# A hybrid retention, RG-LRU and PEER layer on one core: other start addresses for the activation tiles

## The chip, the core and the metric

The kernel runs on one core of a Trainium2 chip. The core has five engines, each with its own instruction queue: TensorE (PE in the profile; its weight loads are PEld), VectorE (DVE), ScalarE (ACT), GpSimd (POOL) and SyncE (SP), which here only issues DMAs. Operands lie in the on-chip memory SBUF, 128 partitions wide; a tile is a range of bytes that begins at the same address in every partition. Matmul results go to PSUM. The metric is the time of one execution on the device in microseconds (us), the median of several runs.

## What is computed

The reference is one layer over 256 tokens of width 2048 with all weights in float32, and a final norm:

```python
def hybrid_layer(h, mem, ...):
    xn = rms_norm(h, mix_norm_g)
    proj = xn @ w_in                                   # 2048 x 6144
    q, k, v, g, xb, yb = jnp.split(proj, ...)
    ret = silu(g) * head_group_norm(chunkwise_retention(rotary(q), rotary(k), v), ret_gn_g)
    lru = rg_lru_group(xb, yb, ...)
    h = h + jnp.concatenate([ret, lru], axis=-1) @ w_out
    h = h + memory_cross_attention(rms_norm(h, ...), rms_norm(mem, ...), w_xq, w_xk, w_xv, w_xo)
    h = h + peer_ffn(rms_norm(h, ffn_norm_g), peer_w_q, peer_sub_keys, peer_u, peer_v)
    return h

def peer_ffn(xn, w_q, sub_keys, u_tab, v_tab):
    sub_scores = ...                                   # 8 heads, 2 halves, 128 keys
    vals, ids = lax.top_k(sub_scores, 16)
    top_sc, pos = lax.top_k(all 256 sums of the two halves, 16)
    eid, gate = ..., softmax(top_sc)                   # 128 experts of 16384 per token
    act = gelu(einsum('td,tkd->tk', x, u_tab[eid]))
    return einsum('tk,tkd->td', gate * act, v_tab[eid])
```

Before it starts, the host only reorders the weights; all arithmetic is on the chip.

## The kernel before

**Float32 products from halves.** Each weight comes in tiles of 128 x 1024 floats (512 KB), loaded by SyncE into a ring of four buffers named `raw`. ScalarE rounds a tile to `hi` (L119, or L1076 in the last part), VectorE computes the remainder `lo` (L120, L1082), and TensorE multiplies both with an activation that is split in the same way. `raw`, `hi` and `lo` lie in the pool `ws` and begin 64 bytes past a multiple of 256.

**Two forms of product.** In `w_mms` (L128 and L131) the weight half is the stationary operand, 128 x 128 at a time, and the activation moves: 512 columns for `hi` (activation high and low part side by side), 256 for `lo`. A block of 128 outputs takes two tiles, 16 + 16 matmuls. `fold` adds the two halves of the result. In `xchunk` (L170 to L172) and `v_mms` (L939 to L941) the activation is stationary and 512 columns of the weight half move, three matmuls for each pair of operands, twelve for a tile.

**The stages, in order of time** (us from the start of the span, with the activation tile that each multiplies):

- 18 to 309: w_in, as 24 blocks for xb, yb and the gate (L128/L131) around 6 chunks for q, k and v (L170 to L172, 109 to 260), all with `xT`. The recurrence and the retention are woven in by `Weave.pump`, a few steps of side work after each weight tile.
- 309 to 517: w_xk (16 blocks) and w_xv (4 chunks) with `mT`.
- 517 to 609: w_out, 4 chunks with `cat`. 609 to 723: w_xq, 16 blocks with `hT`, and the attention. 723 to 822: w_xo, 4 chunks with `oT`.
- 822 to 921: w_pq, 16 blocks with `hT2`; `route` begins on VectorE as side work (top 16 of the scores, for token tile 0 and then 1).
- 921 to 1277: the first 6 chunks of U (L128/L131, 8 blocks each) with `xn`; the end of `route`, then `gbuild` and `compact`, which turn the choice into gate tables (L857 to L875) and lists.
- 1277 to 1898: V chunks 0 to 6 (16 tiles of 12 matmuls, L939 to L941) between the last 6 chunks of U. V multiplies with `ah` and `al`, the high and low part of the gated activations. This part has an order written out by step (`run`): the high half is made three steps ahead, the low half two, the load is issued six ahead.
- 1898 to 2115: V chunks 7 to 10, whose activations lie in `xe`, in the place of `xn`, which is no longer needed. 2115 to 2170: the last V chunk, with `ah` and `al` again, and the final norm.

From 1277 on, the chosen experts that the dense part leaves out are gathered by indirect DMAs from GpSimd (L1119) into a ring of four tiles `gat`, and VectorE multiplies (L1136) and adds (L1144) them as side work.

**What places a tile.** A pool takes its space where the pools before it end, and a tile within it where the tile before it ends, in steps of 32 bytes. The pool `rp` holds `cand`, `eq` and `gs` and ends where `pw` begins, which holds the big activation tiles (`xT`, `cat`, `oT`, `kq`, and above them `lt`, `kv`, `hT2`). Later the pool `pb` takes the place of `pw`: `act`, `foldu`, `key`, `work`, `gsp`, `sel`, `idx`, then `spt`, `spti`, `spi`, `spg`, and last `ah` and `al`. `mT`, `hT`, `xn` and `xe` share one place in the pool `b8`, below `rp`.

**What orders VectorE.** Outside the part with steps, a scheduler of the language orders each engine's instructions by what they depend on, byte range by byte range, starting from the order of the code. `gs` was a tile of its own; `r3` is a view of the tile `rt` whose first row `r3[:, 0]` holds the top values (`vals`) of both score halves, 16 for each of 16 score rows.

## Time and profile before

| | |
|---|---|
| runs | 2168.70, 2173.79, 2179.55 us; median 2173.79 |
| profiled execution | 2172.21 us, of which the span from first to last instruction is 2170.4 |
| mean granted TensorE clock | 0.982 of full speed |
| HBM | 540.94 MB read, 18.87 MB written |
| chain that ended last | TensorE 65%, VectorE 16%, DMA 12%, issue 4%, ScalarE 2% |

The next lines are from the second part of the page, which cuts the span into 40 slices of 54 us. A digit is a share in tenths, 9 is 90% or more; PEclk is the TensorE clock that was granted, DMA the mean busy share of the 16 DMA engines.

```profile
DVE  6847976744554558999987779999999999888885
PEclk9999999999999999999999989999999999999999
DMA  8665555566554457555676579999998999989864
```

VectorE and the DMA engines are far from full in the first half, but for the slices of `route`, and both near full from slice 24 on, where U, V and the gathers run together.

### The profile page before, as it was taken

Reading aid. Unit: us, or ns where it says so; the run is one execution under the profiler, and the core shown is the slowest. Engines: PE = TensorE matmul, PEld = TensorE weight load, DVE = VectorE, ACT = ScalarE, POOL = GpSimd, SP = SyncE. Lnnn points to the kernel's source line nnn. Section 1 sums busy time; section 2 is a strip of 40 time slices with the busy share of each in tenths; the row PEclk is TensorE's granted clock in tenths of the full one; section 3 lists DMA queues with packets and bytes.
Section 4 is the critical chain, followed back from the end, with each engine's and each line's share of the span. In section 5 each row is a group of like instructions: output and inputs, shape, how many; then the busy total and the mean of one; then the engine's idle time right before and its main releaser. Section 6 shows DMA issues by size and latency. Waiting matters only on the chain.

```text
span 2170.4 us, 29029 instructions
## 1 busy us (share of the span) xinstructions
PE 2074.1 (96%) x10452; PEld 1736.4 (80%) x10452; DVE 1702.6 (78%) x2422; ACT 1041.5 (48%) x1592; POOL 357.1 (16%) x210
## 2 busy tenths in 40 slices
PE   8999999999999999999999989989999999988998
PEld 6777788888888888888899878778788777766786
DVE  6847976744554558999987779999999999888885
ACT  6565344444544445454588834443434444333334
POOL 0302221000000000000000013332334233233211
PEclk9999999999999999999999989999999999999999
DMA  8665555566554457555676579999998999989864
GB/s 280 234 211 161 170 170 174 159 193 187 183 167 144 146 176 280 175 178 182 217 231 199 161 288 361 385 356 379 353 336 313 365 387 367 368 337 369 287 214 144
DMA packets 154870, 541.86 MB, mean 250 GB/s; under 512 B 17120, under 2 KB 44384, under 8 KB 136544
## 3 DMA queue, kind: packets, MB, share of 16 engines
q1 hardware_dynamic: 132832, 400.48, 54.5%
q0 software_dynamic: 21888, 139.48, 16.2%
q8 instruction: 82, 1.34, 0.2%
q14 instruction: 68, 0.56, 0.1%
HBM read 540.94 MB, written 18.87 MB: 258 GB/s over the span
## 4 chain that ended last, share of the span: by engine, by line
PE 65%; DVE 16%; DMA 12%; issue 4%; ACT 2%; POOL 0%; DVEq 0%; ACTq 0%; SPq 0%; POOLq 0%
PE U L128 9%; PE wb L128 6%; PE xc L171 6%; PE xc L172 6%; PE xc L170 6%; DMA raw<-in_V_dram 5%; PE U L131 5%; DMA raw<-in_U_dram 5%; PE acc L940 4%; DVE lo L120 4%; PE acc L939 4%; PE acc L941 4%; PE wb L131 3%; DVE lo L1082 3%; PE G L873 2%
## 5 line engine op out<-in xcount | busy, mean ns | idle before, releaser
L120 DVE TENSOR_TENSOR lo<-raw,hi 128x1024 fp32r<-128x1024 f32 x396 | 496.1, 1267 | 265.6 <-PE xc L171 141.0
L119 ACT CAST hi<-raw 128x1024 fp32r<-128x1024 f32 x396 | 415.1, 1050 | 292.8 <-PE xc L172 178.1
L1076 ACT CAST hi<-raw 128x1024 fp32r<-128x1024 f32 x272 | 285.7, 1051 | 410.6 <-DMA raw<-in_V_dram 202.8
L128 PE MATMUL U<-xn,hi 128*128 128x512 f32 x1536 | 383.9, 397 | 9.3 <-DVE foldu L1013 5.0
L1082 DVE TENSOR_TENSOR lo<-raw,hi 128x1024 fp32r<-128x1024 f32 x272 | 328.1, 1220 | 55.9 <-ACT hi L1076 37.8
L128 PEld LDWEIGHTS U<-xn,hi 128*128 128x128 f32 x1536 | 281.7, 190 | 67.5 <-DVE foldu L1013 5.7
L1119 POOL DMA_INDIRECT gat<-in_Us_dram,idx x72 | 123.3, 1713 | 701.7 <-DVE gat L1136 268.2
L131 PE MATMUL U<-xn,lo 128*128 128x256 f32 x1536 | 215.2, 288 | 18.8 <-DVE lo L1082 14.2
L131 PEld LDWEIGHTS U<-xn,lo 128*128 128x128 f32 x1536 | 202.1, 193 | 31.3 <-DVE lo L1082 18.4
L1119 POOL DMA_INDIRECT gat<-in_Vs_dram,idx x72 | 132.3, 1838 | 267.8 <-DVE hh L1144 235.5
L1144 DVE SCALAR_TENSOR_TENSOR hh<-gat,coef,hh 128x2048 f32<-128x2048 f32 x72 | 168.8, 2344 | 0.0
L1136 DVE SCALAR_TENSOR_TENSOR gat<-gat,h 128x2048 f32<-128x2048 f32 x72 | 164.4, 2283 | 0.0
L939 PE MATMUL acc<-hi,ah 128*128 128x512 f32 x384 | 153.0, 398 | 5.0 <-ACT hi L1076 3.4
L940 PE MATMUL acc<-lo,ah 128*128 128x512 f32 x384 | 154.5, 402 | 2.2 <-DVE lo L1082 2.0
L941 PE MATMUL acc<-hi,al 128*128 128x512 f32 x384 | 151.7, 395 | 0.0
L128 PE MATMUL wb<-hT,hi 128*128 128x512 f32 x448 | 113.9, 398 | 0.0
L128 PEld LDWEIGHTS wb<-hT,hi 128*128 128x128 f32 x448 | 81.3, 189 | 15.5
L939 PEld LDWEIGHTS acc<-hi,ah 128*128 128x128 f32 x384 | 72.6, 189 | 24.2 <-ACT hi L1076 3.9
L128 PE MATMUL wb<-xT,hi 128*128 128x512 f32 x368 | 90.3, 396 | 0.1
L940 PEld LDWEIGHTS acc<-lo,ah 128*128 128x128 f32 x384 | 72.7, 189 | 21.9 <-DVE lo L1082 5.2
L941 PEld LDWEIGHTS acc<-hi,al 128*128 128x128 f32 x384 | 72.8, 190 | 17.3
L940 PE MATMUL acc<-lo,xe 128*128 128x512 f32 x192 | 77.1, 401 | 9.7 <-DVE lo L1082 9.7
(404 smaller groups left out, 3659.2 us busy)
## 6 DMA issues: line engine op xcount, KB each, us to landing
raw<-in_U_dram SPq DMA_DIRECT2D x192, 512.0 KB, 5.5
raw<-in_V_dram SPq DMA_DIRECT2D x192, 512.0 KB, 6.0
raw<-in_w_xyg_dram SPq DMA_DIRECT2D x48, 512.0 KB, 4.3
raw<-in_w_qkv_dram SPq DMA_DIRECT2D x48, 512.0 KB, 3.7
raw<-in_w_xk_dram SPq DMA_DIRECT2D x32, 512.0 KB, 3.6
raw<-in_w_xv_dram SPq DMA_DIRECT2D x32, 512.0 KB, 4.4
raw<-in_w_out_dram SPq DMA_DIRECT2D x32, 512.0 KB, 4.0
raw<-in_w_xq_dram SPq DMA_DIRECT2D x32, 512.0 KB, 3.5
```

The costliest lines, as they stand in the source:

```text
L119: A.copy(hi, raw)
L120: V.tensor_tensor(lo, raw, hi.bitcast(F32), op=ALU.subtract)
L128: PE.matmul(pt, hi[:, k * P:(k + 1) * P], xt[:, kb, :], start=(kb == 0), stop=(kb == KB - 1))
L131: PE.matmul(pt[:, :T], lo[:, k * P:(k + 1) * P], xt[:, kb, :T], start=False, stop=False)
L939: PE.matmul(pt, ah[:, c, t_], hi[:, w], start=(first and c == 0), stop=False)
L940: PE.matmul(pt, ah[:, c, t_], lo[:, w], start=False, stop=False)
L941: PE.matmul(pt, al[:, c, t_], hi[:, w], start=False, stop=(last and c == 7))
L1076: A.copy(his[t], raws[t])
L1082: V.tensor_tensor(los[t], raws[t], his[t].bitcast(F32), op=ALU.subtract)
L1119: G.indirect_dma_start(gat, None, a[tab], bass.IndirectOffsetOnAxis(ap=idx[tt][:, k:k + 1], axis=0), bounds_check=NS - 1, oob_is_err=False)
L1136: V.scalar_tensor_tensor(gat, gat, 1.0, h[tt], op0=ALU.mult, op1=ALU.mult, accum_out=dots[tt, k0][:, k:k + 1])
L1144: V.scalar_tensor_tensor(hh[tt], gat, coef[tt, k0][:, k:k + 1], hh[tt], op0=ALU.mult, op1=ALU.add)
```

## The change

Two lines of code change; no arithmetic does. The sums of the gates, 8 floats, move from their own tile into the first 32 bytes of `rt`, and the tile `spg` is made 40 floats long, of which the first two are used as before.

```diff
@@ route()
-            gs = rp.tile([P, 8], F32, tag="gs", name="gs")
+            gs = r3[:, 0, 0, :8]
             V.tensor_reduce(gs, gt, axis=AX.X, op=ALU.add)
             V.reciprocal(gs, gs)
             V.tensor_tensor(gt, gt, gs[:, :, None].to_broadcast([P, 8, 16]), op=ALU.mult)
@@ compact()
-        spl["g"] = tp.tile([P, OV], F32, tag="spg", name="spg")
+        spl["g"] = tp.tile([P, 40], F32, tag="spg", name="spg")[:, :OV]
```

So `rp` ends 32 bytes earlier, and all that lies above it begins 32 bytes lower; the longer `spg` then moves what lies above it in `pb`, `ah` and `al` first of all. The start addresses in the built programs, as bytes past a multiple of 256:

```
tiles                                           before  after
raw, hi, lo; mT, hT, xn, xe; h, hh, gat0..2         64     64
xT, cat, oT, kq; lt, kv, hT2                        96     64
act, foldu, key, work, gsp                          96     64
ah, al                                             224     64
fold, the tiles ro, qk, sT, xp, nrm (tag t2)       160    128
gat3; trio, o1, o2 (the gate tables)                32    128
```

The instructions of TensorE, GpSimd and SyncE stand in the same order as before. On VectorE the scheduler places some of `route` anew, since the first maximum of token tile 1 is written over the bytes where `gs` now lies, and must come after its last use at L728.

The first place is on VectorE during w_pq, in the choice of the top 16 (`sub_6493` are the scores of token tile 0, `sub_6494` those of tile 1, `qp` a block of queries):

```order
 L676 MAX rt<-sub_6494 128x8
 L677 MAX_INDEX rt<-rt,sub_6493 128x8
-L676 MAX rt<-sub_6494 128x8
 L155 TENSOR_TENSOR qp_6488<-wb,fold 128x256
 L676 MAX rt<-sub_6493 128x8
```

One maximum of token tile 1, which stood here long before its index search, is gone from this place.

The second place is on VectorE in the first U blocks, at the end of token tile 0's gates (`foldu` is the sum of a U block, `eq` a table of comparisons):

```order
-L726 TENSOR_REDUCE gs<-rt 128x8
+L726 TENSOR_REDUCE rt<-rt 128x8
 L712 CAST rt<-rt 128x256
-L727 RECIPROCAL gs<-gs 128x8
+L727 RECIPROCAL rt<-rt 128x8
 L926 TENSOR_TENSOR foldu<-U,foldu 128x256
 L720 TENSOR_TENSOR eq<-rt,iota 128x512
-L728 TENSOR_TENSOR rt<-rt,gs 128x128
+L728 TENSOR_TENSOR rt<-rt 128x128
 L722 TENSOR_TENSOR eq<-eq,rt 128x512
-L677 MAX_INDEX rt<-rt,sub_6494 128x8
+L676 MAX rt<-sub_6494 128x8
```

Behind L728, where the index search of token tile 1 stood, now stands its maximum; the index search and what follows it in the same chain come one place later each, between the same low halves for TensorE.

## The prediction

> **What bounds the kernel now.** I began with the page's head, to see which engine could set the time, and then cut the span into the stages of the program (busy time by stretch).

> ```profile
> span 2170.4 us, 29029 instructions
> PE 2074.1 (96%) x10452; PEld 1736.4 (80%) x10452; DVE 1702.6 (78%) x2422; ACT 1041.5 (48%) x1592; POOL 357.1 (16%) x210
> ```

> ```profile
> core 0: us, PE busy (x) PEld busy (x) DVE busy (x) ACT busy (x) POOL busy (x), PEclk, DMA share, GB/s
> 109.00:260.00 151.00, 145.44 (x605) 116.35 (x604) 108.41 (x117) 76.91 (x94) 25.20 (x13) 0.97 0.59 182
> 430.00:517.00 87.00, 87.00 (x386) 72.04 (x385) 39.93 (x34) 38.49 (x41) 0.00 (x0) 1.00 0.63 193
> 517.00:609.00 92.00, 92.00 (x408) 74.45 (x408) 48.08 (x50) 43.46 (x58) 0.00 (x0) 1.00 0.59 183
> 723.00:822.00 99.00, 98.96 (x442) 80.42 (x441) 50.55 (x59) 45.52 (x64) 0.00 (x0) 1.00 0.53 169
> 822.00:921.00 99.00, 98.65 (x582) 86.07 (x581) 93.86 (x253) 53.45 (x93) 1.33 (x2) 1.00 0.65 233
> 921.00:1086.00 165.00, 161.24 (x933) 142.20 (x932) 163.18 (x436) 87.29 (x136) 2.37 (x2) 1.00 0.57 192
> 1277.00:1898.00 621.00, 593.27 (x2879) 488.76 (x2878) 578.95 (x594) 258.76 (x325) 199.06 (x111) 0.99 0.94 359
> 1898.00:2115.00 217.00, 199.50 (x799) 153.91 (x798) 189.05 (x173) 76.17 (x76) 60.41 (x35) 0.96 0.82 303
> 2115.00:2170.00 55.00, 46.10 (x199) 36.76 (x197) 30.63 (x44) 23.52 (x36) 9.65 (x6) 0.96 0.45 145
> ```

> In order the rows are the qkv products (xT), w_xv (mT), w_out (cat), w_xo (oT), w_pq (hT2), the U blocks that run alone, the mixed U and V stage up to V chunk 6, V chunks 7 to 10, and the last V chunk. There are two kinds of stage. In 430:517, 517:609 and 723:822 TensorE is busy without a gap, VectorE about half, DMA about 0.6: there a shorter matmul shortens the stage one for one. In 1277:1898 three things are nearly full at once: TensorE 593 of 621 us, VectorE 579, DMA 0.94 at 359 GB/s. There a shorter matmul may only lengthen a wait.

> The chains of waits by stage agree; in order 109:260, 517:609, 723:822, 1277:1898 and the end:

> ```profile
> by line: PE xc L171 23.4%; PE xc L172 22.9%; PE xc L170 22.7%; DVE lo L120 10.3%; DVE lt L333 7.1%; DMA raw<-in_w_qkv_dram 2.8%; PE gate L321 2.3%; PE gate L320 2.3%; DVE lt L332 2.2%; DVE lt L343 1.2%; POOL lt L334 1.0%; DVE lt L337 1.0%;
> ...
> by line: PE xc L172 32.5%; PE xc L171 32.5%; PE xc L170 32.5%; PE hT L526 2.8%
> ...
> by line: PE xc L172 29.9%; PE xc L170 29.9%; PE xc L171 29.9%; PE xs L573 3.5%; PE xo L599 3.5%; PE hT L526 2.6%; PE xpT L590 0.7%; issue 0.0%
> ...
> by line: DMA raw<-in_U_dram 16.2%; DMA raw<-in_V_dram 11.5%; DVE lo L1082 9.2%; issue 8.5%; PE acc L940 7.7%; PE acc L939 7.2%; PE acc L941 7.0%; PE U L128 6.3%; DMA raw<-gd 3.6%; PE U L131 3.5%; PE V L940 3.1%; PE V L939 3.0%; PE V L941 3.
> ...
> by line: PE acc L939 20.8%; PE acc L941 20.8%; PE acc L940 20.6%; PE V L939 6.7%; PE V L941 6.7%; PE V L940 6.6%; ACT fin L1232 1.3%; ACT hh L1261 1.3%; DVE hh L1251 1.2%; ACTq L1421 1.1%; issue 0.6%; ACT rq_s L182 0.4%; DVE rf L183 0.3%; D
> ```

> **What a start address costs.** No operation is added or taken away; what changes is where operands start. The kernel of before already holds both cases, so its trace can be asked directly. The profile's duration of a matmul is modelled, so I take start to start over 32 matmuls of 512 columns, all products of the same form (weights from the activation tile, weight halves moving). Quoted are the first and last of 32 successive rows of the timeline: w_xv with mT, which starts 64 bytes past a multiple of 256; w_out with cat (96 past); the last V chunk with ah and al (224 past); V chunk 10 with xe (64 past).

> ```profile
> 439.77 0.39 PE L170 MATMUL xc<-hi,mT 128*128 128x512 f32 x1
> ...
> 446.79 0.39 PE L171 MATMUL xc<-lo,mT 128*128 128x512 f32 x1
> ...
> 521.72 0.40 PE L171 MATMUL xc<-lo,cat 128*128 128x512 f32 x1
> ...
> 528.96 0.40 PE L172 MATMUL xc<-hi,cat 128*128 128x512 f32 x1
> ...
> 2118.69 0.40 PE L941 MATMUL acc<-hi,al 128*128 128x512 f32 x1
> ...
> 2125.93 0.40 PE L939 MATMUL acc<-hi,ah 128*128 128x512 f32 x1
> ...
> 2059.82 0.40 PE L941 MATMUL acc<-hi,xe 128*128 128x512 f32 x1
> ...
> 2066.86 0.39 PE L939 MATMUL acc<-hi,xe 128*128 128x512 f32 x1
> ```

> Over 31 intervals that is 7.02 us (226.5 ns each) at 64, 7.24 us (233.5 ns) at 96, 7.24 us (233.5 ns) at 224, and 7.04 us (227.1 ns) at 64 again. The offset goes with 6.4 to 7.0 ns, 3%, in two pairs of stages far apart. After the change all these tiles start 64 past.

> [...]

> In the blocks of the other form (weight halves as weights, activation moving) the chain merges 16 matmuls to a piece:

> ```profile
> 39.35 3.73 PE wb L128 x16
> 43.08 1.87 PE wb L131 x16
> ...
> 927.24 1.91 PE U L131 x16
> 929.15 3.65 PE U L128 x16
> ```

> With xT (96) a block takes 3.73 + 1.87 = 5.60 us; with xn (64) 3.65 + 1.91 = 5.56. The high parts gain 0.08, the low parts lose 0.04.

> **The terms.**

> 1. w_out and w_xo, 4 chunks of 8 tiles of 12 matmuls = 384 each: 384 x 7.0 ns = **2.7 us each**. The chains are 97% and 90% matmuls of just these lines, so all of it is gained. After a chunk's last matmul VectorE and ScalarE are half idle, so nothing else is late.

> 2. qkv, 576 matmuls: 69% of 151 us on the chain is 104 us or 446 matmuls, x 7.0 ns = 3.1 us; for all 576 it would be 4.0. VectorE's low halves and its recurrence (lt) are the next late thing (10.3% and more of the chain), so I take **2.4**, with bounds of 1 and 4.

> 3. Blocks with xT (24) and hT2 (16): 40 x 0.04 = 1.6 us if all were on the chain. In 822:921 VectorE is busy 94 of 99 us, and early blocks wait for DMA; I take **0.4**, bounds 0 and 1.6.

> 4. V chunks 0 to 6 and the last one, which use ah and al. The counts (lines of before; three such lines each):

> ```profile
> L940 PE MATMUL acc<-lo,ah 128*128 128x512 f32 x384 | 154.5, 402 | 2.2 <-DVE lo L1082 2.0
> ...
> L940 PE MATMUL V<-lo,ah 128*128 128x512 f32 x112 | 44.7, 399 | 0.0
> ```

> A chunk has 192 matmuls: 16 tiles of 12. The last: 192 x 6.4 ns = **1.2 us**, all on the chain (the end's row is 82% matmuls). The other seven: 1344 x 6.4 = 8.6 us. Of 621 us the chain has 31% in their lines (21.9% acc, 9.1% V), 192 us or 824 matmuls: 5.3 us if no other path took over. But another one stands right beside it:

> ```profile
> ACT hi L1076 <- DMA raw<-in_V_dram: 124.9, 73, 7.5
> ACT hi L1076 <- DMA raw<-in_U_dram: 109.0, 51, 8.1
> ```

> ScalarE, which makes the high half of each tile, waits 234 us of the 621 for tiles to land, in 124 waits: a saving between two such waits is handed to the second. I take half of 5.3, **2.6**, with bounds of 0 and 8.6.

> 5. The moved maximum. The scheduler issues the first MAX of token tile 1 later, in the U blocks instead of in w_pq, and everything behind it in that chain one place on.

> ```profile
> L676 DVE MAX8 rt<-sub x64: 271/282/300, 869.9 to 1029.0; 128x8 f32<-128x128 f32 x64
> L120 DVE TENSOR_TENSOR lo<-raw,hi 128x1024 fp32r<-128x1024 f32 x396 | 496.1, 1267 | 265.6 <-PE xc L171 141.0
> ```

> It takes 0.28 us out of one stage where VectorE is nearly full and puts it into another (163 of 165 us). Queued behind it are the low halves that TensorE waits for, and the instructions that build the G tables. If the chain ends one slot later, that slot can hold two low halves, 2 x 1.27 = 2.5 us. Bounds -0.3 and +2.5, taken as 0, since the count of instructions is the same. The 8 sums (gs) themselves are written and read by VectorE alone, before and after, so no other engine comes to wait for them.

> 6. Other moved operands. VectorE does not seem to care: the gather ring has three tiles at 64 and one at 32 past, and its 72 products hardly differ:

> ```profile
> L1136 DVE SCALAR_TENSOR_TENSOR gat<-gat,h x72: 2268/2284/2292, 1280.7 to 2044.4; 128x2048 f32<-128x2048 f32 x72
> ```

> The small matmuls that build G (512) move from 32 to 128 past, and no row shows them at 128: by the largest step seen, 7 ns either way, 512 x 7 = 3.6 us, taken as 0 in between.

> Sum: 2.7 + 2.7 + 2.4 + 0.4 + 1.2 + 2.6 = **12.0 us**. The profiled execution, 2172.2 us (1.6 below the median), would be 2160.2; the median of 2173.8 becomes **2161.8**. With every numbered gain at its top it would be 20.8 us; the sure ones (w_out, w_xo, the last chunk) are 6.6.

> **The rivals.**

> *The mixed stage swallows its share, and qkv too.* For it: DMA at 0.94 and the 234 us above. Against: the chain still has 31% of those matmuls. Then only 6.6 plus about 1 remain: 2166. Chance 0.11.

> *The mixed stage passes nearly all on.* VectorE waits for ScalarE, ScalarE for DMA, and a tile is only asked for when its buffer is free, so a faster TensorE could pull the ring along. DMA has 6% of its time left, and needs 1.4% (8.6 of 621). With 8.6 instead of 2.6 and 4.0 for qkv: 2154. Chance 0.10.

> *The start does nothing*; what differs between the stages is who else uses the memory. For it: w_xv has VectorE at 40 of 87 us, w_out at 48 of 92. Against: xe at 64 is fast in a stage where VectorE is at 189 of 217 us, and ah is slow at 31 of 55. Then 2173.8. [...] Chance 0.06.

> *Slower, by the clock.* Where TensorE finishes sooner and waits for the same DMA, its pauses grow. After one such pause the trace shows matmuls at half speed:

> ```profile
> 2018.85 0.73 PE L940 MATMUL acc<-lo,xe 128*128 128x512 f32 x1 [2.29 <-DVE lo L1082]
> ...
> 2021.52 0.63 PE L940 MATMUL acc<-lo,xe 128*128 128x512 f32 x1
> ```

> Six intervals take 2.67 us, 445 ns each. If eight run so (an estimate from these rows), a pause of 2.29 us costs 8 x 0.2 = 1.6 us. To end slower by over 0.5% (10.9 us), with the 9.4 us of the other terms gained, it needs 20.3 / 1.6, about 13 more such pauses; from 6 on, the gain of 9.4 is gone. Against it: in 1277:1898 the clock is at 0.99, and the saving per wait is only 8.6 us over 124 waits, 0.07 us. With 13: 2185. Chance 0.03.

> **How the numbers follow.** A difference of 0.5%, 10.9 us, is about what a measurement of this kernel can tell from none; the line is at 2162.9, one microsecond above my forecast. The forecast has 0.70, of which I put 0.43 beyond the line, since its open terms (2.4 and 2.6) and the spread of the three runs (2168.7 to 2179.55) reach across it. With the rival that passes more on, faster is 0.43 + 0.10 = 0.53; within is 0.27 + 0.11 + 0.06 = 0.44; slower 0.03. The range goes from 2154 (everything passed on) to 2170 (the three sure terms worth half, or the G tables and the moved maximum at their worst).

> **What would show it.** Right: 226 to 227 ns from start to start with xT, cat, oT, ah and al; 5.56 us for blocks with xT and hT2; w_out and w_xo each 2.7 us shorter; the mixed stage shorter by 1 to 5 us, its DMA share up; mean clock as before. Wrong: intervals still at 233 ns (the start does nothing); intervals at 227 but 1277:1898 as long as before (swallowed); a lower granted clock there (the slow rival); waits of TensorE for the G tables (the moved maximum).

## The result, and the profile after

| | before | after |
|---|---|---|
| median | 2173.79 us | 2162.91 us |
| range of 7 runs each | 2165.62 to 2182.10 | 2158.15 to 2164.74 |
| profiled span | 2170.4 | 2161.5 |
| mean granted clock | 0.982 | 0.982 |

The ratio of the times is 0.995, with a 95% interval of 0.9929 to 0.997: 10.9 us less, 6.5 to 15.4. The forecast was 12.0 less, 2161.8 us.

First the intervals, read as before: the first and last of successive rows of TensorE's timeline in the changed kernel, for mT, cat, and ah with al.

```profile
435.83 0.39 PE L171 MATMUL xc<-lo,mT 128*128 128x512 f32 x1
...
442.86 0.39 PE L172 MATMUL xc<-hi,mT 128*128 128x512 f32 x1
...
517.66 0.39 PE L172 MATMUL xc<-hi,cat 128*128 128x512 f32 x1
...
524.91 0.39 PE L171 MATMUL xc<-lo,cat 128*128 128x512 f32 x1
...
2111.67 0.39 PE L941 MATMUL acc<-hi,al 128*128 128x512 f32 x1
...
2118.92 0.39 PE L940 MATMUL acc<-lo,ah 128*128 128x512 f32 x1
```

These are 32, 33 and 33 matmuls, so 7.03 / 31, 7.25 / 32 and 7.25 / 32 us: 227 ns in all three. Before, the second and third had 233.5. The other form changed as its two pieces said: in the chain of the changed kernel a block with xT is now a pair of pieces of 3.65 and 1.91 us, as with xn; at the same place the low part, with 256 columns moving, is the slower one, 1.91 us for 1.87 with xT at 96.

```profile
279.28 1.91 PE wb L131 x16
281.20 3.65 PE wb L128 x16
```

Then the stages. A stage here runs from its first matmul to the first of the next; both come from the rows of the timeline, and differences are taken before rounding. Next are busy times by stretch, of the changed kernel, with its own boundaries: w_out, w_xo, the mixed stage and the last V chunk.

```profile
core 0: us, PE busy (x) PEld busy (x) DVE busy (x) ACT busy (x) POOL busy (x), PEclk, DMA share, GB/s
513.80:603.60 89.80, 89.80 (x410) 74.62 (x409) 48.53 (x51) 43.21 (x58) 0.00 (x0) 1.00 0.62 187
716.50:814.10 97.60, 97.49 (x445) 80.99 (x444) 50.82 (x59) 45.82 (x64) 0.00 (x0) 1.00 0.57 172
1269.30:1889.70 620.40, 588.88 (x2880) 491.28 (x2881) 579.24 (x596) 260.11 (x326) 195.97 (x111) 0.99 0.95 360
2108.00:2161.00 53.00, 44.18 (x196) 36.19 (x194) 29.19 (x44) 23.50 (x36) 10.13 (x6) 0.97 0.46 149
```

| stage | before | after | difference |
|---|---|---|---|
| w_in blocks ahead of qkv | 100.7 | 106.7 | +6.1 |
| qkv | 152.1 | 145.2 | -6.9 |
| w_xk (mT, not moved) | 121.1 | 117.9 | -3.3 |
| w_xv (mT, not moved) | 87.3 | 87.3 | 0.0 |
| w_out | 92.2 | 89.7 | -2.5 |
| w_xo | 99.8 | 97.6 | -2.2 |
| mixed, V chunks 0 to 6 | 621.7 | 620.4 | -1.3 |
| last V chunk and the end | 54.4 | 53.1 | -1.3 |

w_out, w_xo and the last chunk do what the sum said. The first three rows do not, and one profile cannot tell a change from an execution that went otherwise. The mixed stage is the place to look for what became of the saving: before, over 1276.6 to 1898.3, the same view has

```profile
1276.60:1898.30 621.70, 593.97 (x2881) 489.34 (x2882) 579.62 (x597) 259.16 (x325) 199.06 (x111) 0.99 0.94 359
```

TensorE's busy time fell by 5.1 us, the stage by 1.3. ScalarE's waits in the changed kernel (1269 to 1890) come next; the last row is its wait for TensorE to free a buffer.

```profile
ACT hi L1076 <- DMA raw<-in_V_dram: 139.1, 77, 8.0
ACT hi L1076 <- DMA raw<-in_U_dram: 111.4, 55, 6.9
...
ACT hi L1076 <- PE acc L941: 7.5, 5, 2.3
```

Before, that row read

```profile
ACT hi L1076 <- PE acc L941: 28.9, 16, 2.7
```

In this pair ScalarE waits 250.5 us for tiles where it waited 233.9, and 7.5 us for TensorE at this line where it waited 28.9. It would be easy to read that as the place where the saving went: TensorE lets go of its buffers sooner, and the tile that is to come next is not there. The profile of a second execution, described with the experiments, does not bear it out (1267 to 1886):

```profile
ACT hi L1076 <- DMA raw<-in_V_dram: 125.2, 74, 7.1
ACT hi L1076 <- DMA raw<-in_U_dram: 103.2, 51, 6.5
...
ACT hi L1076 <- PE acc L941: 16.7, 8, 4.0
```

There ScalarE waits 228.4 us for tiles, less than before. The extra wait for tiles was the first execution's own.

### The profile page after: what moved, and what is told of

Read it like the earlier page. It is cut to its first block, busy times and chain, and to the rows that moved or that the text cites. A ratio compares the mean times of both kernels' runs of the same rounds, so it can differ in the third digit from the quotient of the medians.

```text
span 2161.5 us, 29029 instructions
## 1 busy us (share of the span) xinstructions
PE 2058.6 (95%) x10452; PEld 1739.3 (80%) x10452; DVE 1700.6 (79%) x2422; ACT 1042.0 (48%) x1592; POOL 354.8 (16%) x210
## 3 DMA queue, kind: packets, MB, share of 16 engines
q0 software_dynamic: 21888, 139.48, 16.2%
## 4 chain that ended last, share of the span: by engine, by line
PE 65%; DVE 17%; DMA 11%; issue 3%; ACT 2%; POOL 1%; DVEq 0%; ACTq 0%; SPq 0%; POOLq 0%
PE U L128 9%; PE wb L128 7%; PE xc L171 6%; PE xc L172 6%; PE xc L170 6%; DMA raw<-in_V_dram 5%; PE U L131 5%; DVE lo L120 4%; PE wb L131 4%; DMA raw<-in_U_dram 4%; PE acc L940 4%; PE acc L941 4%; PE acc L939 4%; DVE lo L1082 3%; PE G L873 2%
## 5 line engine op out<-in xcount | busy, mean ns | idle before, releaser
L120 DVE TENSOR_TENSOR lo<-raw,hi 128x1024 fp32r<-128x1024 f32 x396 | 493.4, 1260 | 263.1 <-PE xc L171 136.2
L1076 ACT CAST hi<-raw 128x1024 fp32r<-128x1024 f32 x272 | 285.6, 1051 | 411.5 <-DMA raw<-in_V_dram 223.5
L128 PE MATMUL U<-xn,hi 128*128 128x512 f32 x1536 | 386.9, 399 | 11.0 <-DVE foldu L1013 5.3
L1082 DVE TENSOR_TENSOR lo<-raw,hi 128x1024 fp32r<-128x1024 f32 x272 | 327.9, 1220 | 53.9 <-ACT hi L1076 41.0
L128 PEld LDWEIGHTS U<-xn,hi 128*128 128x128 f32 x1536 | 284.6, 192 | 69.3 <-DVE foldu L1013 5.1
L131 PE MATMUL U<-xn,lo 128*128 128x256 f32 x1536 | 215.0, 288 | 19.1 <-DVE lo L1082 13.8
L131 PEld LDWEIGHTS U<-xn,lo 128*128 128x128 f32 x1536 | 202.1, 193 | 31.2 <-DVE lo L1082 17.4
L1136 DVE SCALAR_TENSOR_TENSOR gat<-gat,h 128x2048 f32<-128x2048 f32 x72 | 164.5, 2284 | 0.0
L940 PE MATMUL acc<-lo,ah 128*128 128x512 f32 x384 | 152.3, 397 | 4.2 <-DVE lo L1082 4.1
L939 PE MATMUL acc<-hi,ah 128*128 128x512 f32 x384 | 151.0, 393 | 5.0 <-ACT hi L1076 4.1
L941 PE MATMUL acc<-hi,al 128*128 128x512 f32 x384 | 150.6, 392 | 0.0
L128 PE MATMUL wb<-hT,hi 128*128 128x512 f32 x448 | 113.0, 396 | 0.0
L128 PEld LDWEIGHTS wb<-hT,hi 128*128 128x128 f32 x448 | 81.4, 189 | 14.8
L940 PEld LDWEIGHTS acc<-lo,ah 128*128 128x128 f32 x384 | 72.7, 189 | 25.1 <-DVE lo L1082 10.1
L128 PE MATMUL wb<-xT,hi 128*128 128x512 f32 x368 | 91.9, 402 | 0.7 <-ACT hi L119 0.7
L939 PEld LDWEIGHTS acc<-hi,ah 128*128 128x128 f32 x384 | 72.7, 189 | 21.1 <-ACT hi L1076 4.5
L940 PE MATMUL acc<-lo,xe 128*128 128x512 f32 x192 | 77.8, 405 | 9.0 <-DVE lo L1082 9.0
L941 PEld LDWEIGHTS acc<-hi,al 128*128 128x128 f32 x384 | 72.7, 189 | 14.8
```

The source lines that it names most:

```text
L120: V.tensor_tensor(lo, raw, hi.bitcast(F32), op=ALU.subtract)
L128: PE.matmul(pt, hi[:, k * P:(k + 1) * P], xt[:, kb, :], start=(kb == 0), stop=(kb == KB - 1))
L131: PE.matmul(pt[:, :T], lo[:, k * P:(k + 1) * P], xt[:, kb, :T], start=False, stop=False)
L939: PE.matmul(pt, ah[:, c, t_], hi[:, w], start=(first and c == 0), stop=False)
L940: PE.matmul(pt, ah[:, c, t_], lo[:, w], start=False, stop=False)
L941: PE.matmul(pt, al[:, c, t_], hi[:, w], start=False, stop=(last and c == 7))
```

## The experiments

One theory and its rivals were open. The theory: the saving follows from the start addresses alone, and is gained in full where TensorE bounds the stage, in part in qkv and in the mixed stage. Its rivals: the new order on VectorE has a share in it; the mixed stage swallows its part, by DMA or by VectorE; and, on the addresses themselves, that a multiple of 64 is what counts, and not the same place as the weight halves.

**The order of the routing.** `gs` lies in `ss1`, 8 floats that are no longer used then.

```diff
-            gs = rp.tile([P, 8], F32, tag="gs", name="gs")
+            gs = ss1.rearrange("p a b -> p (a b)")
-        spl["g"] = tp.tile([P, OV], F32, tag="spg", name="spg")
+        spl["g"] = tp.tile([P, 40], F32, tag="spg", name="spg")[:, :OV]
```

> All tiles start where they do after the change, but the 8 gate sums lie in another small tile that is idle by then, so that VectorE's order in the routing is that of before. If the addresses alone make the gain, it is 9 to 12 us faster than before, and within 2 us of the change. If the new order of the routing costs or gives something, it differs from the change by that, at most 2.5 us.

Measured: 2163.11 us, ratio to before 0.9958 (0.9942 to 0.9975), 9.1 us less. The change itself on the same chip had 2162.45. The 0.7 us between them is far inside the spread of each (12 executions over 10 and 14 us), so the times alone would not exclude a cost of 2.5 us. The stages say more: w_pq and the U blocks up to 1277, where the moved maximum and all that follows it lie, take 98.8 and 356.4 us, and 99.0 and 357.6, in the two profiles of the change, and 98.6 to 99.7 and 355.3 to 357.7 in the eight whole kernels with the old order. The new order has no share that can be seen; the addresses carry the gain.

**One part at a time.** For the big tiles alone, `gs` in `ss1` and `spg` 16 floats long; for ah and al alone, `gs` as before and `spg` 32 floats long. With ah and al go the gate tables and gat3, from 32 to 128.

```diff
-        spl["g"] = tp.tile([P, OV], F32, tag="spg", name="spg")
+        spl["g"] = tp.tile([P, 16], F32, tag="spg", name="spg")[:, :OV]
...
-        spl["g"] = tp.tile([P, OV], F32, tag="spg", name="spg")
+        spl["g"] = tp.tile([P, 32], F32, tag="spg", name="spg")[:, :OV]
```

> xT, cat, oT and hT2 start 64 past a multiple of 256, ah and al stay at 224. My sum gives 2.7 + 2.7 + 2.4 + 0.4 = 8.2 us faster than before, matmul intervals of 226.5 ns in w_out and w_xo and 233.5 ns in the V chunks with ah. If qkv hands its share on, 5 to 6 us. If the mixed stage is what made the gain, under 3 us.

> Only ah and al start 64 past, xT, cat, oT and hT2 stay at 96. My sum gives 1.2 + 2.6 = 3.8 us faster than before; if the mixed stage swallows its share, 1 to 2 us; if it passes it on, 8 to 10 us. Intervals of 227 ns in the V chunks, 233.5 in w_out and w_xo.

Measured: the big tiles alone 2163.42 us, ratio 0.9965 (0.995 to 0.9981), 7.6 us less (4.1 to 10.9); ah and al alone 2167.47 us, ratio 0.998 (0.9964 to 0.9996), 4.3 us less (0.9 to 7.8). The sums had said 8.2 and 3.8. The intervals follow the part that was moved: with only ah and al moved, 227 ns in the V chunks with them and 233 in w_out; with only the big tiles moved, 233 and 227. The result for ah and al is too wide to say how much of it is the mixed stage: take the 1.2 us of the last chunk off, and 0 to 6.6 is left.

**The change again.**

> The changed kernel itself, beside the other three on one chip: 9 to 12 us faster than before. A second profile of it shows how far the lengths of single stages vary between executions: the w_in blocks, which took 6 us longer in the first profile of it, and the qkv stage, 7 us shorter, should come out the other way about as often.

Measured: 2162.45 us, ratio 0.9962 (0.9947 to 0.9977), 8.3 us less (5.0 to 11.5). Its w_in blocks took 101.3 us, not 106.7, and qkv 145.1. So the 6 us of the w_in blocks were that one execution's. The short qkv stage did not come out the other way: it came again.

**Which start.** A pad of 8 floats in the lowest pool puts weight halves and activations at 96, all of them; or the tile of the gate sums is 64 bytes long.

```diff
     ones = cp.tile([P, P], F32, name="ones")
+    cp.tile([P, 8], F32, name="pad")
...
-            gs = rp.tile([P, 8], F32, tag="gs", name="gs")
+            gs = ss1.rearrange("p a b -> p (a b)")
-        spl["g"] = tp.tile([P, OV], F32, tag="spg", name="spg")
+        spl["g"] = tp.tile([P, 40], F32, tag="spg", name="spg")[:, :OV]
```

```diff
-            gs = rp.tile([P, 8], F32, tag="gs", name="gs")
+            gs = rp.tile([P, 16], F32, tag="gs", name="gs")[:, :8]
```

> A small tile more at the bottom, so that the weight halves and every activation tile start 96 past a multiple of 256: all at one place, but none at a multiple of 64. If what counts is that both operands start at the same place, every interval is 226.5 ns and the time that of the change. If each operand must start at a multiple of 64, intervals are 233 ns or more everywhere, also with mT, xn and xe, and the time is 5 to 25 us above before.

> The tile of the gate sums is 64 bytes long in place of 32: xT, cat, oT and hT2 start at 128, ah and al at 0 past a multiple of 256, weight halves at 64 as before. If a multiple of 64 is enough, intervals are 226.5 ns with all of them and the time 9 to 12 us below before. If the same place as the weight halves is needed, they stay at 231 to 237 ns and the time is that of before.

Two rows of the timeline each: w_out of the kernel with everything at 96 (32 matmuls; its lines are one higher), w_out of the one with cat at 128 (32 matmuls), and the last V chunk of that one, with ah and al at 0 (33 matmuls).

```profile
513.79 0.39 PE L172 MATMUL xc<-lo,cat 128*128 128x512 f32 x1
...
520.82 0.39 PE L173 MATMUL xc<-hi,cat 128*128 128x512 f32 x1
```

```profile
520.75 0.40 PE L172 MATMUL xc<-hi,cat 128*128 128x512 f32 x1
...
527.99 0.39 PE L170 MATMUL xc<-hi,cat 128*128 128x512 f32 x1
```

```profile
2120.65 0.39 PE L941 MATMUL acc<-hi,al 128*128 128x512 f32 x1
...
2127.98 0.39 PE L940 MATMUL acc<-lo,ah 128*128 128x512 f32 x1
```

7.03 / 31 is 226.8 ns with both at 96, which is no multiple of 64; 7.24 / 31 is 233.5 ns with 128 against 64, both multiples of 64. What counts in these runs is that both operands start at the same place: 227 ns with both at 64, 226.8 with both at 96. The third, 7.33 / 32, is 229.1 ns, which neither expectation gave: 0 against 64 costs 2.3 ns over 226.8, a third of the 6.7 that 128 against 64 does. The times: 2152.76 us, once, and 2171.97, once, beside 2171.23 for before. The first was ten below the change, with the same intervals, so it was timed again:

> The kernel with every operand at 96 past a multiple of 256 again, timed. Its one time was 2152.8 us, ten below the change, though its matmuls come at the same intervals of 227 ns. If the ten are real, the median is 2150 to 2156 us; if that was one lucky execution, it is 2160 to 2165 us, as with the change.

Measured: 2165.09 us, ratio 0.9949 (0.9929 to 0.9968), the seven runs from 2157.61 to 2170.32. The ten were one execution. Its mixed stage had taken 614.9 us; in the second profile of the same kernel, 627.4.

**How often places repeat.** The tile of the gate sums is 256 bytes long: the big tiles are 256 bytes from the weight halves' place, ah and al 128.

```diff
-            gs = rp.tile([P, 8], F32, tag="gs", name="gs")
+            gs = rp.tile([P, 64], F32, tag="gs", name="gs")[:, :8]
```

> The tile of the gate sums is 256 bytes long: xT, cat, oT and hT2 start 256 bytes further up than in the change, ah and al 128 bytes further up; weight halves stay at 64. If places repeat every 256 bytes, w_out and w_xo keep their 226.5 ns and take 89.7 and 97.5 us; if only every 512, they are at 230 ns or more. With 128 of difference, ah and al show 227 ns if places repeat every 128 bytes, 230 to 237 ns if not.

```profile
516.75 0.39 PE L171 MATMUL xc<-lo,cat 128*128 128x512 f32 x1
...
523.78 0.39 PE L172 MATMUL xc<-hi,cat 128*128 128x512 f32 x1
...
2115.83 0.39 PE L940 MATMUL acc<-lo,ah 128*128 128x512 f32 x1
...
2122.80 0.40 PE L940 MATMUL acc<-lo,ah 128*128 128x512 f32 x1
```

32 rows and 31 rows: 226.8 ns for cat, 232.3 for ah and al. Here a distance of 256 bytes, at 226.8 ns, is as good as none; one of 128, at 232.3, is not. w_out took 89.7 us and w_xo 97.6, as in the change; the last chunk 54.2, about as with ah at 224. The kernel took 2167.32 us, once.

**What swallows the mixed stage's saving.** Two pairs, each with the addresses of before and of the change: without the gathers' DMAs (VectorE's products stay, on zeroed tiles), and with the gathers but products over 8 of 2048 columns. Both leave out the gathered experts, so only their stages are compared.

```diff
         turn[0] += 1
-        G.indirect_dma_start(gat, None, a[tab], bass.IndirectOffsetOnAxis(ap=idx[tt][:, k:k + 1], axis=0),
-                             bounds_check=NS - 1, oob_is_err=False)
         return gat
```

```diff
-        V.scalar_tensor_tensor(gat, gat, 1.0, h[tt], op0=ALU.mult, op1=ALU.mult,
+        V.scalar_tensor_tensor(gat[:, :8], gat[:, :8], 1.0, h[tt][:, :8], op0=ALU.mult, op1=ALU.mult,
...
-        V.scalar_tensor_tensor(hh[tt], gat, coef[tt, k0][:, k:k + 1], hh[tt], op0=ALU.mult, op1=ALU.add)
+        V.scalar_tensor_tensor(hh[tt][:, :8], gat[:, :8], coef[tt, k0][:, k:k + 1], hh[tt][:, :8], op0=ALU.mult, op1=ALU.add)
```

> Leaves out the gathers' DMAs (VectorE works on the four zeroed ring tiles instead), addresses of before. It is the base for the next run. The mixed stage (V chunks 0 to 6, 621 us) should shorten to 585 to 605 us, since DMA has half as much to move, if DMA bounds it.

> The same without the gathers' DMAs, addresses of the change. If DMA is what swallows the saving in the mixed stage, that stage is now 5 to 8.6 us shorter than in the run with the addresses of before. If VectorE is what swallows it, the difference stays at 0 to 2 us, as with the gathers.

> VectorE's two products for each gathered row work on 8 of 2048 columns; the gathers' DMAs stay. Addresses of before, the base for the next run. VectorE then has some 200 us less to do in the mixed stage of 621 us. If DMA bounds the stage, it shortens by less than 30 us; if VectorE bounds it, by far more.

> The same with the addresses of the change. Without the gathers' DMAs the mixed stage gave 6.8 of the 8.6 us that shorter matmuls could give there. If DMA alone swallows the saving, the difference to the run before it is 0 to 2 us in that stage, though VectorE is half idle. If VectorE is what swallows it too, the difference is 4 us or more.

The mixed stage by stretch in the four, in this order, each a view of its own:

```profile
1270.40:1864.70 594.30, 586.06 (x2881) 488.06 (x2882) 578.52 (x597) 257.95 (x327) 0.00 (x0) 1.00 0.62 198
```

```profile
1266.00:1853.50 587.50, 577.74 (x2881) 488.13 (x2882) 577.29 (x597) 257.50 (x326) 0.00 (x0) 1.00 0.62 200
```

```profile
1274.40:1884.60 610.20, 590.58 (x2881) 492.13 (x2881) 353.05 (x597) 258.87 (x326) 144.44 (x112) 0.99 0.96 367
```

```profile
1268.00:1858.30 590.30, 579.34 (x2880) 491.16 (x2881) 353.07 (x597) 259.53 (x325) 144.21 (x112) 0.99 0.97 379
```

Without the gathers' DMAs the stage is 27 us shorter (594.3 for 621.7), though VectorE has as much to do as before, and there the aligned matmuls give 6.8 us of the 8.6 that my sum gave them there (an estimate, 1344 matmuls x 6.4 ns). That fits DMA as what swallows the saving, but it does not prove it: with the transfers the edit takes out GpSimd's work and every wait for a gathered row, each kernel ran once, and the stage of whole kernels differs by more than 6.8 us between executions. The second pair does not decide on VectorE. With 227 us less work for VectorE the stage shortens by 11.5 us, and between the two addresses by 19.9, more than twice those 8.6 us; DMA moved 367 GB/s in the one execution and 379 in the other, 3%, with its engines at 0.96 and 0.97. By the line drawn beforehand (4 us or more) this speaks for VectorE as well, but one execution each can't say how much of the 19.9 is the change's.

## Why the prediction was right

Stage lengths of all profiles of whole kernels, by where the stage's activation tiles stood to the weight halves:

| | same place | other place |
|---|---|---|
| w_out | 89.7 to 89.8 (7 profiles) | 92.2 (3) |
| w_xo | 97.5 to 97.6 (7) | 99.8 (3) |
| qkv | 145.1 to 147.9 (7) | 149.3 to 152.1 (3) |
| last V chunk | 53.1 to 53.2 (6) | 53.5 to 54.4 (4) |
| mixed stage | 614.9 to 627.4 (6) | 621.0 to 623.9 (4) |
| TensorE busy in the mixed stage | 585.5 to 592.4 (6) | 592.8 to 594.4 (4) |

1. *w_out and w_xo, 2.7 us each*: the mechanism is right and the size a little high; 2.5 and 2.2. The 226.5 ns that I took was a little low, 227 is nearer.

2. *qkv, 2.4 us, bounds 1 and 4*: right. The means of the seven and the three are 146.5 and 150.3, a difference of 3.8; with the two pairs that leave the gathers out, which are whole up to there, 146.7 of nine and 149.5 of five, 2.8. The single pair's 6.9 was too much by an execution's own share.

3. *Blocks with xT and hT2, 0.4*: the block is 0.04 us shorter, as the two pieces said. It stays below what the stages can show: w_pq takes 98.8 us for 99.0, and the w_in blocks ahead of qkv have means of 102.1 (the seven) and 101.8 (the three).

4. *The V chunks with ah and al*: 1.2 us for the last one is right to a tenth (54.4 to 53.1). The 2.6 for the mixed stage stay the one term that I can't confirm. The means of the six and the four are 621.0 and 622.4 us, 1.4 less, but the stage spreads over 12 us between two executions of one kernel, and ah and al alone gave 4.3 us (0.9 to 7.8) in all. That a part of the 8.6 us is lost again shows on TensorE, over the same ten profiles: the means of its busy time are 589.6 and 593.8 us, 4.2 less, and those of its idle time (length less busy time) 31.5 and 28.6, 2.9 more. Which wait takes it is not shown; the pair without the gathers' DMAs fits DMA, and no more.

5. *The moved maximum, 0*: right as far as the stages of `route` show, by the kernels with the old order.

6. *Other moved operands, 0*: right for the matmuls that build G. With the tables at 32 (before) and at 128 (after) their rows are

```profile
L873 PE MATMUL G<-o,o 128*128 128x96 f32 x512 | 68.0, 273 | 1.0 <-ACT o L863 1.0
...
L873 PE MATMUL G<-o,o 128*128 128x96 f32 x512 | 68.4, 274 | 1.0 <-ACT o L863 1.0
```

The forecast of 12.0 us was somewhat high, and that the first comparison came within 1.1 us of it is partly luck: the second, with more executions, gave 8.3 (5.0 to 11.5). By the stages, w_out, w_xo and the last chunk gave 6.0 of 6.6, and the means of qkv and the mixed stage 2.8 and 1.4.

The rival of the clock did not come as a slower kernel: the mixed stage has 0.99 in both profiles. In small it may have come: counting matmuls of the mixed stage that follow the one before, with no wait, at 1.4 times the full-speed interval or more (227 ns with 512 columns moving, some 119 with 256), the traces have 50 before and 72 and 73 in the two profiles of the change, some 3 us more. But the kernel with everything at 96 has 55 in one execution and 82 in the other, so that is not shown to be the change's. The rival that the start does nothing is out: with its start, cat went from 233.5 to 227 ns.

Why the distance between the two starts matters (for cat 227 ns at 0 or 256 bytes, 233.5 at 32 and at 64) was not tried.

One thing in the reasoning was looser than it read: the two cases in the trace of before, 64 against 96 and 224, could not tell "a good start" from "the same start". Both gave the same number for this change, and different ones for the kernels at 96 and at 128.

## What to carry to other kernels

Where a stage is bound by back-to-back matmuls of 512 float32 columns, look at where its two operands start: here 3% of each matmul went away (227 ns for 233.5) when the stationary and the moving tile began at the same place or 256 bytes apart, and the number could be read beforehand, since one stage, w_xv, already had it (226.5 ns). With 256 columns moving, the same place was the slower one (1.91 against 1.87 us for 16 matmuls), so measure the form that bounds the stage. Multiply the saving by the matmuls on the chain of waits, not by all: 6 us in three stages were sure, and the rest lay in stages that also wait for VectorE, ScalarE and DMA. And look at more than one profile before a stage's length is put down to a change, where that stage waits for DMA: the mixed stage of one kernel took 614.9 and 627.4 us.

- With the weight halves at 64, activations whose start is 0 or 256 bytes from that place run at 227 ns; cat 32 and 64 bytes from it runs at 233.5, ah 128 and 160 bytes from it at 232.3 and 233.5. With both at 64 the interval is 227 ns, with both at 96 it is 226.8. Not all distances cost the same: with ah 64 bytes below, the interval was 229.1 ns and the last chunk lay between, at 53.5 us.
- The same mixed stage took 614.9 us in one execution and 627.4 in another of the same kernel, at 363 and 355 GB/s.
- w_xk, where neither mT nor the weight halves moved against each other, takes 117.7 to 117.9 us, 119.4 to 119.7 or 121.1 to 121.5. The longest pause of TensorE in it is the same, 3.8 to 3.9 us, but the granted clock is not, 0.94 to 0.99. Over 306 to 428, before, with everything at 96 (the execution of 2152.76 us), and after:

```profile
306.00:428.00 122.00, 114.03 (x647) 98.72 (x647) 89.97 (x151) 52.66 (x72) 20.35 (x11) 0.94 0.48 150
```

```profile
306.00:428.00 122.00, 113.67 (x647) 98.10 (x646) 88.17 (x146) 53.32 (x72) 17.54 (x9) 0.96 0.49 154
```

```profile
306.00:428.00 122.00, 113.11 (x661) 97.75 (x661) 93.24 (x153) 53.67 (x74) 18.94 (x11) 0.99 0.50 155
```

So 3.3 of the 9 us between the two profiled executions go with the granted clock, 0.94 against 0.99. Whether the change has a part in this is open, and no term of the sum covers it: all six profiles with the big tiles where the change puts them have 117.7 to 117.9, the four with them where they were before have 117.7, 119.4, 121.1 and 121.2. That both operands start at the same place is not enough for it: the kernel with the big tiles 256 bytes further up has 121.2.
